# A two-layer decoder step: the score weights and 24 more expert blocks split by ScalarE and GpSimd during the scores

## The chip, the core and the metric

The kernel runs on one core of a Trainium2 chip. The metric is the device time of one execution in microseconds (us). In the profile PE is TensorE's matmul, PEld its weight load, DVE VectorE, ACT ScalarE, POOL GpSimd and SP SyncE, which issues most DMAs.

## What is computed

One inference step of two trunk layers over 512 prompt tokens and 8 sample tokens of width 1024, in float32. Each layer is a token mixer, then a layer norm, then a PEER layer (a mixture of 16384 tiny experts) and a second layer norm. Layer 0 mixes by a gated DeltaNet and an RG-LRU, layer 1 by sliding-window attention. The change lies in PEER:

```python
def block(tb):                                   # 128 tokens
    q = (tb @ w_q).reshape(PEER_BLOCK, PEER_HEADS, 2, PEER_D_SUB)
    s = jnp.einsum('thcd,hcnd->thcn', q, sub_keys).astype(F32)
    s_top, i_top = lax.top_k(s, PEER_TOPK)
    cand = (s_top[:, :, 0, :, None] + s_top[:, :, 1, None, :]).reshape(PEER_BLOCK, PEER_HEADS, -1)
    cand_idx = (i_top[:, :, 0, :, None] * PEER_N_KEYS + i_top[:, :, 1, None, :]).reshape(
        PEER_BLOCK, PEER_HEADS, -1)
    best, pos = lax.top_k(cand, PEER_TOPK)
    expert = jnp.take_along_axis(cand_idx, pos, axis=-1)
    gate = jax.nn.softmax(best, axis=-1)
    act = jax.nn.gelu(jnp.einsum('td,thkd->thk', tb, u_tab[expert]).astype(F32))
    return jnp.einsum('thk,thkd->td', (gate * act).astype(tb.dtype), v_tab[expert])
```

## The kernel before

A float32 product is done in float16 with a **pair**: `hi` is the scaled value rounded to float16 and `lo` the remainder, and `mm3` makes three matmuls, hi by hi, hi by lo and lo by hi. `split` (L73) makes a pair of a block: ScalarE writes `hi` (L71) and VectorE computes `scale * src - hi` in one operation (L80). `wblock` (L89) loads a weight block of 128 by 1024 into a `wst` buffer (three of them) and splits it into `wh` and `wl` (two of each).

`peer` (L271) handles one layer. Three token tiles of 128 (384 tokens) go through TensorE against all 16384 experts, 128 blocks of 128 experts; the fourth tile and the samples (136 columns) gather only the experts chosen. Its stages, in the order of the program:

- **Scores** (L358 to L410). For each of 16 blocks of `wq`: 48 matmuls into `pq`, a copy `q` to SBUF, matmuls against the keys into `psc`, a copy `scs`, and VectorE's top 16 of 128 (`topk_half`).
- **Pairs** (`topk_pairs`, L225). For a list of tokens the sums of the two halves' best are laid out as 50 candidates (`cand`, and `ce` for their expert numbers): 16 operations of VectorE for `cand` and 33 for `ce` (L238, L242), then the top 16 of 50 and a lookup (`eq`). There are six such lists in a layer: the samples, two halves of the gather tile, and three dense tiles.
- **u blocks** (`u_step`, L305). A block of `u` is multiplied with the 384 tokens (24 matmuls into `pu`), and ScalarE applies gelu (`act`). The first 16 blocks of layer 0 (12 of layer 1) were split during the mixer and kept as pairs in DRAM (`PW`, `presplit` L98, `NPRE`); `ublock` (L112) loads those as `wpr` and splits the others through `wblock`. 79 blocks are multiplied before the products with `v` begin.
- **Gather** (L337, L344). GpSimd gathers rows of `u` (36 of 136 in this stretch), and VectorE multiplies and sums each against a token (`hd`, L346).
- **Gates** (L454). For each 32 tokens VectorE builds one-hot rows `oh`, 64 matmuls make `pg`, ScalarE copies them into `stage`, and a DMA of 2 MB writes `GD`; twelve times, with u blocks between.
- **Products** (L613 to L650). 128 blocks of `v` with the gated activations into `yps`, with the rest of the u blocks and gathers between.

The program is built by a scheduler that orders each engine's instructions by a modelled time. So work of a later list, or u blocks, can stand on an engine ahead of work that comes earlier in the text. Once built, the order of each engine is fixed, and an instruction that waits holds up all behind it on its engine.

Of the kernel before, what the change touches and what calls it, by code (L numbers as in the profile page):

```python
# [18 lines left out]
P = 128  # L19
D = 1024  # L20
PB, PC = 4, 2
KB = 8                      # blocks of 128 along d_model
NP = 512                    # prompt tokens
NS = 8                      # sample tokens
NT = NP + NS
ND = 384                    # prompt tokens whose experts go through the tensor engine
W5 = 3 + NP + 4 * NS        # padded sequence of the causal convs
C5 = W5 - 3                 # its outputs
S5 = NP + 3                 # first sample's output column in it (step 4)
# [7 lines left out]
def lookup_order():  # L37
    """pairs (a, b), (a + 1)(b + 1) <= 16, by blocks of product <= 4, 8, 12, 16: segments (a, b0, b1),
    pairs up to each block, and each pair's place in the a-major order of the candidates"""
    start = np.concatenate([[0], np.cumsum([TOPK // (a + 1) for a in range(TOPK)])])  # L40
    seg, cnt, perm = [], [], []
    for hi in (4, 8, 12, 16):
        for a in range(hi):
            b0, b1 = (hi - 4) // (a + 1), hi // (a + 1)
            if b1 > b0:
                seg.append((a, b0, b1))
                perm += [start[a] + b for b in range(b0, b1)]
# [5 lines left out]
SCW = 1024.0                # exact power-of-two scales of the float16 pairs  # L53
# [3 lines left out]
LSC = 8.0 * SQK * SQK       # of the attention's logits  # L57
# [7 lines left out]
class Kern:  # L65
# [3 lines left out]
    # ---------------------------------------------------------------- helpers  # L69
# [3 lines left out]
    def split(self, hi, lo, src, scale=1.0, eng=None):  # L73
        """hi + lo = scale * src, both float16"""
# [7 lines left out]
    def mm3(self, out, wh, wl, xh, xl, start, stop):  # L82
        """out += w^T x of float16 pairs"""
# [5 lines left out]
    def wblock(self, src, lo=None):  # L89
        """one 128-column block of a weight, [128 d, 8, 128] in DRAM, as a scaled float16 pair"""  # L90
# [4 lines left out]
        self.split(h, l, st, SCW, lo)  # L95
        return h, l

    def presplit(self, pool, layer, n):  # L98
        """the first n blocks of u as float16 pairs in DRAM, while a mixer runs"""
# [11 lines left out]
    def ublock(self, layer, b):  # L111
        if b < self.NPRE[layer]:  # L112
# [5 lines left out]
    def proj_block(self, ps, w):  # L118
        """ps[128, 2, 512] (256 + 264 columns) = SCW * w^T x^T"""
# [7 lines left out]
    # ---------------------------------------------------------------- constants  # L127
# [15 lines left out]
    # ---------------------------------------------------------------- layer norm  # L143
# [6 lines left out]
    def layer_norm(self, pool, r, out, gb, n):  # L150
        """out = LN(ALPHA * r) for n tokens on partitions, by halves"""
# [17 lines left out]
    def to_xT(self, psum, src, t, n, tag="s"):  # L169
        """columns of tile t (n tokens) of x^T as a float16 pair"""  # L170
# [1488 lines left out]
```

## Time and profile before

| | |
|---|---|
| device time, 3 runs | 3040.98 us median (3040.34 to 3042.37) |
| span of the profiled execution | 3044.4 us (no other time of it is known) |
| TensorE busy | 2877.3 us, 95% |
| VectorE busy | 2562.9 us, 84% |
| ScalarE busy | 1315.2 us, 43% |
| GpSimd busy | 842.1 us, 28% |
| scores of layer 0 | 368 to 470 us |
| pairs and u blocks of layer 0, up to the first gate matmul | 470 to 625 us |
| gates of layer 0 | 625 to 845 us |
| products of layer 0 | 876 to 1545 us |
| the same points of layer 1 | 1827, 1930, 2098, 2321, 2352, 3034 us |

A row of a group tells line, engine, operation, what it writes and reads, its shape and count, then the engine's busy time and the mean of one, then the idle time just before them and what ended most of it. In a timeline a row has its start, its length and, in brackets, the idle time of its engine before it and what ended that. Matmuls are pipelined: the distance of two starts, not the length, is what one costs.

### The profile page before, as it was taken

The page shows a single profiled execution, that of the slowest core. Times are in us where ns is not written, and L with a number is a line of the kernel's source. Part 1 is how long each engine was busy: PE and PEld are TensorE (multiplying, and loading weights), DVE is VectorE, ACT ScalarE, POOL GpSimd, SP SyncE. Part 2 cuts the span into 40 slices and gives each one's busy share as a digit, 9 for nine tenths or more (in the row PEclk, how much of TensorE's full clock was granted, in tenths as well). Part 3 has the DMA queues.
Part 4 walks back from the last instruction along what each step waited for, and adds up shares of the span by engine and source line. Part 5 has one row for each costly group of instructions (what it writes and reads, how often), then busy time and mean ns, then how long its engine had stood idle before and what let it go on. Part 6 is the DMA issues. An engine that isn't in the chain of part 4 may idle for free.

```text
span 3044.4 us, 49637 instructions
## 1 busy us (share of the span) xinstructions
PE 2877.3 (95%) x18246; PEld 1756.8 (58%) x18246; DVE 2562.9 (84%) x5816; ACT 1315.2 (43%) x2149; POOL 842.1 (28%) x661
## 2 busy tenths in 40 slices
PE   8989999899999999999987899989999999999998
PEld 7787596466655555544455558645665555554443
DVE  6775699999878888899874758989987898888998
ACT  4753232366743333333335633334665333333332
POOL 2300102300045555336410000131001545444552
PEclk9999999999999999999998899999999999999999
DMA  4273326866699999999959512586558999999996
GB/s 134 70 252 112 122 78 223 293 210 214 229 373 374 369 355 364 363 362 365 349 175 231 177 57 91 169 300 223 208 208 307 387 365 357 352 358 354 366 355 239
DMA packets 331689, 798.60 MB, mean 262 GB/s; under 512 B 28515, under 2 KB 164843, under 8 KB 327604
## 3 DMA queue, kind: packets, MB, share of 16 engines
q1 hardware_dynamic: 242832, 444.75, 43.6%
q0 software_dynamic: 78336, 285.25, 25.3%
q10 hardware_dynamic: 10276, 65.43, 5.8%
q8 instruction: 143, 2.34, 0.3%
q14 instruction: 102, 0.84, 0.1%
HBM read 700.89 MB, written 93.10 MB: 261 GB/s over the span
## 4 chain that ended last, share of the span: by engine, by line
PE 61%; DMA 12%; DVE 11%; issue 8%; ACT 6%; POOL 1%; SPq 0%; ACTq 0%; DVEq 0%; POOLq 0%
PE yps L587 30%; PE pu L87 6%; PE pu L86 6%; PE pu L85 6%; DMA GD<-stage 4%; ACT stage L71 3%; DMA row<-in_u_rows,elist 2%; DMA pst<-in_uT 2%; DVE wl L80 2%; DVE row L346 1%; DMA bd<-bt 1%; ACT wh L71 1%; PE pq L85 1%; PE pq L87 1%; PE pq L86 1%
## 5 line engine op out<-in xcount | busy, mean ns | idle before, releaser
L587 PE MATMUL yps<-vv,vw 128*128 128x512 f16 x4536 | 1009.9, 379 | 11.6 <-ACT vv L71 9.9
L587 PEld LDWEIGHTS <-vw 128*128 128x128 f16 x4608 | 450.3, 98 | 543.9 <-issue 17.5
L87 PE MATMUL pu<-xh,wl 128*128 128x384 f16 x1824 | 599.3, 329 | 36.6 <-DVE wl L80 36.2
L339 POOL DMA_INDIRECT row<-in_v_rows,elist x272 | 383.5, 1410 | 891.8 <-ACT stage L71 452.0
L85 PE MATMUL pu<-xh,wh 128*128 128x384 f16 x1824 | 599.7, 329 | 15.7 <-ACT act L315 11.7
L86 PE MATMUL pu<-xl,wh 128*128 128x384 f16 x1824 | 599.6, 329 | 0.0
L71 ACT ACTIVATE wh<-wst 128x1024 f16<-128x1024 f32 x296 | 312.4, 1056 | 606.8 <-PE pu L86 347.7
L339 POOL DMA_INDIRECT row<-in_u_rows,elist x272 | 385.6, 1418 | 674.4 <-DVE hd L346 133.4
L80 DVE SCALAR_TENSOR_TENSOR wl<-wst,wh 128x1024 f16<-128x1024 f32 x296 | 361.2, 1221 | 200.3 <-ACT wh L71 184.7
L87 PEld LDWEIGHTS <-wl 128*128 128x128 f16 x2912 | 288.0, 99 | 186.6 <-DVE wl L80 49.3
L86 PEld LDWEIGHTS <-wh 128*128 128x128 f16 x2912 | 288.2, 99 | 165.9 <-issue 32.0
L85 PEld LDWEIGHTS <-wh 128*128 128x128 f16 x2912 | 290.5, 100 | 158.4 <-ACT wh L71 23.6
L71 ACT ACTIVATE vv<-row 128x1024 f16<-128x1024 f32 x252 | 262.8, 1048 | 222.7 <-PE yps L587 174.7
L525 DVE SCALAR_TENSOR_TENSOR yac<-row,wgt,yac 128x1024 f32<-128x1024 f32 x268 | 343.1, 1280 | 4.3 <-DMA row<-in_v_rows,elist 1.3
L80 DVE SCALAR_TENSOR_TENSOR vv<-row,vv 128x1024 f16<-128x1024 f32 x252 | 307.4, 1221 | 46.3 <-ACT vv L71 41.4
L346 DVE CUSTOM_DVE_ANT_0 row<-row,xtok 128x1024 f32<-128x1024 f32 x256 | 308.5, 1219 | 18.5 <-DMA row<-in_u_rows,elist 18.5
L71 ACT ACTIVATE vw<-act 128x384 f16<-128x384 f32 x256 | 129.8, 516 | 370.4 <-PE yps L587 307.6
L71 ACT ACTIVATE stage<-pg 128x512 f32<-128x512 f32 x192 | 183.4, 1104 | 72.1 <-DMA GD<-stage 67.4
L78 DVE TENSOR_TENSOR vw<-act,vw 128x384 f16<-128x384 f32 x256 | 139.6, 553 | 24.9 <-ACT vw L71 23.3
L315 ACT ACTIVATE act<-pu 128x384 f32<-128x384 f32 x256 | 122.4, 478 | 54.6 <-PE pu L87 41.2
L85 PE MATMUL pq<-xh,wh 128*128 128x264 f16 (+1 forms) x512 | 142.0, 277 | 0.0
L86 PE MATMUL pq<-xl,wh 128*128 128x264 f16 (+1 forms) x512 | 141.9, 277 | 0.0
(482 smaller groups left out, 3997.5 us busy)
## 6 DMA issues: line engine op xcount, KB each, us to landing
row<-in_v_rows SPq DMA_DIRECT2D x256, 512.0 KB
wst<-in_uT SPq DMA_DIRECT2D x228, 512.0 KB
GD<-stage ACTq DMA_DIRECT2D x24, 2048.0 KB
gl<-GD SPq DMA_DIRECT2D x64, 768.0 KB
wst<-in_wq SPq DMA_DIRECT2D x32, 512.0 KB
pst<-in_uT SPq DMA_DIRECT2D x56, 256.0 KB
PW<-ppr SPq DMA_DIRECT2D x56, 256.0 KB
wpr<-PW SPq DMA_DIRECT2D x28, 512.0 KB
```

What stands on the lines that cost most here:

```text
L71: self.nc.scalar.activation(out, in_, AF.Copy, scale=scale)
L78: eng.tensor_sub(lo, src, hi)
L80: eng.scalar_tensor_tensor(lo, src, scale, hi, op0=OP.mult, op1=OP.subtract)
L85: mm(out, wh, xh, start=start, stop=False)
L86: mm(out, wh, xl, start=False, stop=False)
L87: mm(out, wl, xh, start=False, stop=stop)
L315: S.activation(t, ps[:, 0:ND], AF.Gelu_apprx_tanh, scale=1.0 / SCW)
L339: G.indirect_dma_start(out=r, out_offset=None, in_=src, in_offset=bass.IndirectOffsetOnAxis(ap=elist[:, k:k + 1], axis=0))
L346: V.tensor_tensor_reduce(u, u, self.xtok[:, 0] if k < P else xrep, 1.0, 0.0, OP.mult, OP.add, hd[:, k:k + 1])
L525: V.scalar_tensor_tensor(dst, vbuf.pop(n), wgt[:, k:k + 1], dst, op0=OP.mult, op1=OP.add)
L587: T.matmul(yps[t][:, o], w[:, a, c], v[:, b, o], start=x == 0 and k == 0, stop=x == P - 1 and k == 2)
```

## The change

`psplit` is a second way to make a pair. ScalarE writes `hi`, ScalarE scales the source in place, and GpSimd subtracts. All 16 score blocks (`qblock`) use it. During the scores, `presplit_pool` does the same to 24 more blocks of `u`, one or two after each score block: a load of 512 KB into `gst`, two copies of ScalarE, a subtraction of GpSimd, and a DMA of the pair `gpr` to `PW`. So 40 blocks of layer 0 (36 of layer 1) come from DRAM as pairs instead of 16 (12). `sums` lays out the candidates with operations that cover several rows of a: 7 for `cand` and 20 for `ce`.

```diff
+                if seg and seg[-1][1:] == (a, b0, b1):
+                    seg[-1] = (seg[-1][0], a + 1, b0, b1)
+                else:
+                    seg.append((a, a + 1, b0, b1))
...
+CSEG = [(a0, a1, 0, TOPK // a1) for a0, a1 in ((0, 1), (1, 2), (2, 3), (3, 4), (4, 5), (5, 8), (8, 16))]
...
-        self.split(h, l, st, SCW, lo)
+        if lo:
+            self.psplit(h, l, st)
+        else:
+            self.split(h, l, st, SCW)
         return h, l
 
+    def psplit(self, hi, lo, src):
+
+        self.copy(hi, src, SCW)
+        self.copy(src, src, SCW)
+        self.nc.gpsimd.tensor_sub(lo, src, hi)
+
+    def presplit_pool(self, pool, layer, b):
+
+        nc = self.nc
+        st = pool.tile([P, KB, P], F32, name="gst", bufs=2)
+        nc.sync.dma_start(st, self.A["uT"][layer, b])
+        o = pool.tile([P, 2, KB, P], F16, name="gpr", bufs=2)
+        self.psplit(o[:, 0], o[:, 1], st)
+        nc.sync.dma_start(self.PW[layer, b], o)
...
-        if b < self.NPRE[layer]:
+        if b < self.NPRE[layer] + self.NPOOL:
...
-        for a in range(TOPK):
-            nb = TOPK // (a + 1)
-            V.tensor_add(cand[:n, :, off:off + nb], st[:, 0, :, a:a + 1].to_broadcast([n, H, nb]), st[:, 1, :, 0:nb])
-            off += nb
-        off = 0
-        for a, b0, b1 in LSEG:
-            V.tensor_add(ce[:n, :, off:off + b1 - b0], fx[:n, 0, :, a:a + 1].to_broadcast([n, H, b1 - b0]),
-                         fx[:n, 1, :, b0:b1])
-            off += b1 - b0
+
+        def sums(out, x, segs):
+
+            off = 0
+            for a0, a1, b0, b1 in segs:
+                s = [n, H, a1 - a0, b1 - b0]
+                o = out[:n, :, off:off + s[2] * s[3]].rearrange("p h (a b) -> p h a b", a=s[2])
+                V.tensor_add(o, x[:n, 0, :, a0:a1, None].to_broadcast(s), x[:n, 1, :, None, b0:b1].to_broadcast(s))
+                off += s[2] * s[3]
+
+        sums(cand, st, CSEG)
+        sums(ce, fx, LSEG)
...
+            def qblock(hc):
+                return self.wblock(A["wq"][layer, hc], True)
...
-                        wb = self.wblock(A["wq"][layer, hc + 2])
+                        wb = qblock(hc + 2)
...
+                while npool[0] < self.NPOOL * (hc + 1) // 16:
+                    self.presplit_pool(tp, layer, self.NPRE[layer] + npool[0])
+                    npool[0] += 1
...
-            self.NPRE = (16, 12)
-            self.PW = dp.tile([2, max(self.NPRE), P, 2, KB, P], F16, name="PW")
+            self.NPRE, self.NPOOL = (16, 12), 24
+            self.PW = dp.tile([2, max(self.NPRE) + self.NPOOL, P, 2, KB, P], F16, name="PW")
```

The scheduler lays the instructions out anew. ScalarE in the middle of layer 0's scores, one score block before the change (`q` and `scs` are the copies of the projections and of the scores):

```order
L71 ACTIVATE wh<-wst 128x1024
L71 ACTIVATE q<-pq 128x256
L71 ACTIVATE q<-pq 128x264
L71 ACTIVATE scs<-psc 128x512
L71 ACTIVATE ss<-psc 128x8
```

and the same place after it, up to the next block's `wh`:

```order
L76 ACTIVATE wh<-wst 128x1024
L76 ACTIVATE q<-pq 128x256
L76 ACTIVATE q<-pq 128x264
L76 ACTIVATE gst<-gst 128x1024
L76 ACTIVATE scs<-psc 128x512
L76 ACTIVATE ss<-psc 128x8
L76 ACTIVATE wst<-wst 128x1024
L76 ACTIVATE gpr<-gst 128x1024
L76 ACTIVATE gst<-gst 128x1024
L76 ACTIVATE wh<-wst 128x1024
```

The in-place scaling of the score block stands behind the copies of the block before, and one or two u blocks stand between two score blocks.

SyncE's queue at the end of layer 0's scores, before (`wpr` loads a pair, `AD` stores a finished activation):

```order
L92 DMA wst<-in_wq 128x1024 x16
L114 DMA wpr<-PW 128x2048 x4
L317 DMA AD<-act 128x384
L114 DMA wpr<-PW 128x2048
L317 DMA AD<-act 128x384
```

and after (`gst` loads a block to be split, `PW<-gpr` stores it):

```order
L137 DMA wpr<-PW 128x2048
L119 DMA PW<-gpr 128x2048
L116 DMA gst<-in_uT 128x1024
L119 DMA PW<-gpr 128x2048
L116 DMA gst<-in_uT 128x1024
L137 DMA wpr<-PW 128x2048
L119 DMA PW<-gpr 128x2048
L116 DMA gst<-in_uT 128x1024
L342 DMA AD<-act 128x384
L119 DMA PW<-gpr 128x2048
L137 DMA wpr<-PW 128x2048
L342 DMA AD<-act 128x384
```

The loads of the first u blocks now stand behind stores that wait for GpSimd's subtractions.

VectorE ahead of the first one-hot rows `oh` of layer 0, before (`ISA` is the dot product of a gathered row):

```order
L441 CAST ij<-e_6600 128x256
L231 CAST fx_8914<-ix 128x256
L223 MAX_INDEX pos_7757<-best_7756,cwork 128x8
L80 SCALAR_TENSOR_TENSOR wl<-wst,wh 128x1024
L351 TENSOR_TENSOR wgt<-wgt,glist 128x8
L232 TENSOR_SCALAR fx_8914<-fx_8914 128x128
L221 MATCH_REPLACE cwork<-best_7756,cand_7705 128x50
L346 ISA row,hd<-row,xtok 128x1024
L346 ISA hd 128x1
L80 SCALAR_TENSOR_TENSOR wl<-wst,wh 128x1024
L222 MAX best_7756<-cwork 128x8
L448 TENSOR_SCALAR lt<-pt 128x128
```

and after:

```order
L470 TENSOR_SCALAR e_6688<-ei 128x128
L471 TENSOR_SCALAR e_6688<-ei 128x128
L254 CAST fx_8892<-ix 128x256
L244 MATCH_REPLACE cwork<-best_7746,cand_7717 128x50
L371 ISA row,hd<-row,xtok 128x1024
L371 ISA hd 128x1
L473 CAST ij<-e_6688 128x256
L255 TENSOR_SCALAR fx_8892<-fx_8892 128x128
L245 MAX best_7746<-cwork 128x8
L246 MAX_INDEX pos_7747<-best_7746,cwork 128x8
```

The splits `wl` are gone from this place, and work of the next lists stands in theirs.

## Rows read from the trace of the kernel before

**Rows 1.** The page: the span, and busy time by engine

```profile
span 3044.4 us, 49637 instructions
...
PE 2877.3 (95%) x18246; PEld 1756.8 (58%) x18246; DVE 2562.9 (84%) x5816; ACT 1315.2 (43%) x2149; POOL 842.1 (28%) x661
```

**Rows 2.** Busy time by stretch: start:end, length, engines, granted clock, DMA share, GB/s

```profile
368.12:470.00 101.88, 101.88 (x920) 91.49 (x919) 88.13 (x525) 32.41 (x76) 0.00 (x0) 0.99 0.25 79
470.00:625.20 155.20, 138.08 (x813) 79.95 (x811) 142.50 (x635) 49.75 (x76) 49.49 (x38) 0.97 0.82 280
625.20:845.30 220.10, 214.78 (x1799) 146.21 (x1799) 203.83 (x405) 150.19 (x186) 1.87 (x2) 0.99 0.61 215
845.30:876.10 30.80, 24.84 (x142) 13.76 (x140) 19.08 (x22) 16.13 (x23) 8.73 (x6) 0.94 1.00 369
876.10:1545.00 668.90, 662.82 (x3339) 326.10 (x3337) 599.73 (x774) 251.48 (x357) 326.32 (x227) 1.00 1.00 361
1930.00:2098.00 168.00, 147.61 (x861) 85.06 (x860) 153.89 (x657) 55.72 (x83) 50.04 (x38) 0.97 0.78 266
2098.00:2320.90 222.90, 211.03 (x1759) 142.30 (x1757) 197.27 (x387) 147.64 (x183) 2.85 (x3) 0.99 0.60 210
2320.90:2352.20 31.30, 28.73 (x164) 16.04 (x164) 21.14 (x24) 18.42 (x26) 7.30 (x5) 0.95 0.98 367
```

**Rows 3.** Timeline of TensorE around one stall: start, length, engine, line, op, operands, [idle before]

```profile
569.28 0.33 PE L86 MATMUL pu<-xl,wh 128*128 128x384 f16 x1
...
570.26 0.33 PE L86 MATMUL pu<-xl,wh 128*128 128x384 f16 x1
575.76 0.50 PE L87 MATMUL pu<-xh,wl 128*128 128x384 f16 x1 [5.18 <-DVE wl L80]
576.06 0.52 PE L85 MATMUL pu<-xh,wh 128*128 128x384 f16 x1
```

**Rows 4.** The same stall on ScalarE and VectorE

```profile
572.33 1.06 ACT L71 ACTIVATE wh<-wst 128x1024 f16<-128x1024 f32 x1 [5.19 <-DMA wst<-in_uT]
...
572.42 1.23 DVE L346 CUSTOM_DVE_ANT_0 row<-row,xtok 128x1024 f32<-128x1024 f32 x1 [4.38 <-DMA row<-in_u_rows,elist]
```

**Rows 5.** VectorE, 470 to 625 us: groups; busy, mean ns, idle before

```profile
L346 DVE CUSTOM_DVE_ANT_0 row<-row,xtok 128x1024 f32<-128x1024 f32 x28 | 33.8, 1217 | 8.0 <-DMA row<-in_u_rows,elist 8.0
L80 DVE SCALAR_TENSOR_TENSOR wl<-wst,wh 128x1024 f16<-128x1024 f32 x17 | 20.6, 1214 | 1.8 <-ACT wh L71 1.8
...
L242 DVE TENSOR_TENSOR ce<-fx 128x8 f32<-128x8 f32 x53 | 5.6, 169 | 0.0
```

**Rows 6.** Who waited for whom, 470 to 625 us: total us, times, longest

```profile
PE pu L87 <- DVE wl L80: 13.4, 6, 5.6
...
ACT wh L71 <- DMA wst<-in_uT: 7.9, 3, 5.2
```

**Rows 7.** ScalarE, 368 to 470 us: groups

```profile
L71 ACT ACTIVATE wh<-wst 128x1024 f16<-128x1024 f32 x14 | 14.8, 1057 | 59.7 <-PE pq L86 59.7
L71 ACT ACTIVATE scs<-psc 128x512 f32<-128x512 f32 x15 | 9.0, 599 | 0.3 <-PE psc L390 0.3
L71 ACT ACTIVATE q<-pq 128x264 f32<-128x264 f32 x16 | 6.1, 383 | 0.0
```

**Rows 8.** GpSimd, whole span: its largest writes and smallest operations

```profile
L698 POOL MEMSET wbd<- 128x1024 f32 x1 | 1.0, 951 | 0.0
...
masks.py:199 POOL TENSOR_SCALAR_AFFINE_SELECT ident<-ident 128x128 f32<-128x128 f32 x1 | 0.3, 288 | 0.0
...
L1632 POOL MEMSET const-float32-0.0<- 128x1 f32 x1 | 0.1, 104 | 0.3 <-issue 0.3
```

**Rows 9.** GpSimd's copies of the conv state beside VectorE's two-operand split

```profile
L826 POOL COPY cs<-xp x16: 183/972/1188, 29.0 to 152.4; 128x3 f32<-128x3 f32 x16
...
64.67 0.97 POOL L826 COPY cs<-xp 128x3 f32<-128x3 f32 x1 [5.85 <-ACT xp L71]
...
64.38 1.23 DVE L80 SCALAR_TENSOR_TENSOR wl<-wst,wh 128x1024 f16<-128x1024 f32 x1 [1.61 <-ACT wh L71]
```

More of the change, by code (lines that the diff above doesn't have):

```diff
@@ L45, in lookup_order @@
             if b1 > b0:
-                seg.append((a, b0, b1))
+                if seg and seg[-1][1:] == (a, b0, b1):
+                    seg[-1] = (seg[-1][0], a + 1, b0, b1)
+                else:
+                    seg.append((a, a + 1, b0, b1))
                 perm += [start[a] + b for b in range(b0, b1)]
@@ L234, in topk_pairs @@
         ce = pool.tile([P, HM, NC50], F32, name="ce%d" % HM)[:, 0:H]
-        off = 0
-        for a in range(TOPK):
-            nb = TOPK // (a + 1)
-            V.tensor_add(cand[:n, :, off:off + nb], st[:, 0, :, a:a + 1].to_broadcast([n, H, nb]), st[:, 1, :, 0:nb])
-            off += nb
-        off = 0
-        for a, b0, b1 in LSEG:
-            V.tensor_add(ce[:n, :, off:off + b1 - b0], fx[:n, 0, :, a:a + 1].to_broadcast([n, H, b1 - b0]),
-                         fx[:n, 1, :, b0:b1])
-            off += b1 - b0
+        def sums(out, x, segs):
[7 more added lines that the diff above has]
+        sums(ce, fx, LSEG)
         best = pool.tile([P, HM, TOPK], F32, name="best%d" % HM)[:, 0:H]
@@ L371, in proj @@
                 return ps
-            wb = self.wblock(A["wq"][layer, 0])
+            def qblock(hc):
+                return self.wblock(A["wq"][layer, hc], True)
+            wb = qblock(0)
             ps = proj(wb)
-            wb = self.wblock(A["wq"][layer, 1])
+            wb = qblock(1)
+            npool = [0]
             for hc in range(16):
```

## The prediction

> **What bounds the kernel now.** I read the page first, then the busy times by stretch, then the waits and one stall in the timeline. TensorE is busy 2877.3 us of a span of 3044.4 us [rows 1], so a gain can only come from where it stops or runs slowly. In the scores it never stops: 101.9 of 101.9 us. In the products it stops for 6.1 of 668.9 us. What it leaves idle lies between: 17.1 us of the pairs stretch of layer 0 (155.2 less 138.1), 20.4 us in layer 1, 5.3 and 11.9 us in the gates, 6.0 and 2.6 us between the last gate and the first product [rows 2]. To that comes the clock: in both pairs stretches the granted clock is 0.97 [rows 2], so 3% of 155.2 and of 168.0 us, 4.7 and 5.0 us, go to matmuls at the lower level. One stall shows both. TensorE stands still for 5.18 us, waiting for `wl`, the VectorE part of a u block's split, and its next matmuls start 0.30 us apart where six steps before the stall took 0.98 us, 0.163 us each [rows 3]. VectorE is the engine that is late there: it is busy for 142.5 of 155.2 us [rows 2], and 17 splits are 20.6 us of it [rows 5]. But the same stall has a second cause: ScalarE had waited 5.19 us for the block's load, and VectorE 4.38 us for a gathered row [rows 4]. Over the stretch TensorE waited 13.4 us for `wl` and ScalarE 7.9 us for loads [rows 6]. The whole room in the six places is 63.3 us idle and 9.7 us of clock, 73 us. The profiled execution's span is 3.4 us above the median of the runs, 3041.0 us. Nothing else of that execution's own time is known, so I take gains in its microseconds off the median.
>
> **Pairs stretch: the u splits.** The 24 blocks per layer now come as pairs, so TensorE waits there for a load alone. In the new order no split `wl` is left on VectorE ahead of the first one-hot; in layer 0 there were 17, 20.6 us. Ahead of that point stand 113 candidate sums where 196 stood; at 0.169 us [rows 5] the 83 less save 14.0 us. The new sums cover the same elements with more dimensions, which no row prices; at the cost of the old ones apiece the saving is 14.0 us, and at double it would be none. And 27 dots stand ahead instead of 35: eight times 1.217 us [rows 5] is 9.7 us that moves behind. So VectorE has 142.5 - 44.3 = 98 us before the first one-hot, and with the 8.0 us that it waits for rows [rows 5] it would be there at 470 + 106 = 576 us. TensorE is the later one: the new order has 672 u matmuls ahead of the first gate matmul (794 before; layer 1: 683 and 842), 672 x 0.163 = 110 us from 470 us, and with 8 us of waits 588 us, against 625 us before. It has then 122 matmuls, 20 us, less behind it, so the true gain is what it no longer waits. Layer 0: 13.4 us of waits for `wl` and 4.7 us of clock are 18.1 us. The late loads stay: of the 7.9 us on ScalarE [rows 6] I leave 4 us to TensorE, and 14 us are gained. Between what ends: 0, if every stall is a late load, and 21.8 us, if all idle time and the clock come back. Layer 1 has 25.4 us of idle and clock; in the same ratio, 14 of 21.8, it gains 16 us. **Sum 30 us.**
>
> **Gates and the way to the products.** VectorE's work in the gates stays about as it was: 5 splits (6.1 us) and two lists with 22 sums less each (7.4 us) go, 8 dots (9.7 us) come, of 203.8 us [rows 2]. TensorE has 20 us more to do there, and so fewer holes: of 17.2 us idle I take 4 us back; the ends are -6 (VectorE late with the dots) and 17. Behind the last gate stand 168 u matmuls instead of 139 in layer 0, and 150 instead of 164 in layer 1. They cover the store and reload of the gates: 29 x 0.163 = 4.7 us more cover and 2.3 us less. **Plus 2 us.**
>
> **Scores: what comes.** TensorE sets a block's period here, 101.9 / 16 = 6.37 us [rows 2], so whatever fits under it costs nothing. ScalarE gets 14 scalings of `wst` and about 22 pairs of copies; at 1.057 us each [rows 7] that is 58 x 1.057 = 61 us on top of 32.4 us [rows 2], 94 of 101.9 us. It fits by 8 us, in an order where every instruction waits for the one ahead. GpSimd gets 16 + 22 = 38 subtractions of 128 x 1024. No row shows one. The lower end is its write of that size, 0.95 us. For the upper end, an operation that reads 128 elements takes 288 ns and the smallest 104 ns, so 184 ns go to 128 elements; 1024 make 1.47 us, and two operands at twice that with 0.1 us of start 3.05 us [rows 8]. Between 0.95 and 3.05 I take 2.4 us, nearer to the row that reads. Then GpSimd has 38 x 2.4 = 91 us of work in 101.9 us, and from the moment a block's buffers come free `wh` (1.06), two `q` (0.38 each), perhaps a `gst` copy (1.06), `scs` (0.60), the scaling (1.06) and the subtraction (2.4) make 6.9 us, about one period. So ScalarE and GpSimd are both some 90% full, and now and then `wl` comes late. I take 3 us per layer, between 0 and 21 us (38 x 3.05 = 116 us, 14 above the period, and half a period of waiting in turn). SyncE's queue holds the first loads of u behind stores that wait for GpSimd; the old order put 16 score loads and four pairs in a row. Up to two subtractions, 4.8 us, can be late there, which is inside these ends. The first gathers stand behind GpSimd's last subtractions, but wait for the first list anyway. **Minus 6 us.** The 24 MB more of loads and stores per layer go into a stretch with 0.25 of the DMA used [rows 2] and hide there.
>
> [...]
>
> **The sum.** 30 + 4 + 2 - 6 = 30 us: 3041 - 30 = **3011 us**. Nothing is changed in the mixers and the products, which I cost at nothing.
>
> **Rivals.** *Everything hides.* GpSimd is quick, scores cost nothing, and the pairs stretch loses all its idle time and clock: 21.8 + 25.4, with half of the other 25.8 us, are 60 us, 2981 us. For it speaks that `wl` is the wait named; against it the late loads in the same stall.
>
> *VectorE and GpSimd shut each other out.* The trace shows one direction: a copy of GpSimd that takes 0.18 us alone took 0.97 us when VectorE's split of two SBUF operands had begun 0.29 us before it, and it ended with that split [rows 9]. If it also holds the other way, a VectorE operation with two operands waits for a whole subtraction. By the new order 27 sums of the first half of the gather tile stand in the middle of the scores, with subtractions all around. At 2.4 us each they take 65 us. VectorE has 13.8 us free there [rows 2] and 17 us from the splits that left: it falls 34 us behind if nothing brakes it, and 19 us if its three `scs` buffers stop ScalarE, and with it GpSimd, after three blocks. The first one-hot then comes at 595 to 610 us instead of 588, and each layer loses 7 to 22 us: 3025 to 3055 us, in the middle 3040 us. Against it: the top-16 operations, most of VectorE's work there, read one operand.
> [...]
>
> *GpSimd sets the scores (slower).* If a subtraction takes more than 101.9 / 38 = 2.7 us, GpSimd becomes the bound of the scores, and each 0.1 us above costs 3.8 us per layer. The other terms give 36 us, so from (101.9 + 18) / 38 = 3.15 us on the kernel is slower than before. At 3.6 us it costs 35 us per layer: 3041 - 36 + 70 = 3075 us. Mixed types (float32 less float16, into float16) and waits for VectorE speak for it; the rows end at 3.05 us.
>
> *Late loads keep the stalls.* The u loads in the pairs stretch share the DMA with 36 gathers, at 0.82 of the DMA and 280 GB/s where 361 is the most of a long stretch [rows 2]; the stretch gets shorter and its bytes hardly fewer. Then the splits leave and the stalls stay: 8 us of the 30 are gained, 3033 us.
>
> **How the numbers follow.** Forecast 0.46, everything hides 0.18, shut out 0.14, GpSimd bound 0.15, late loads 0.07. A measurement of this kernel tells about 0.2%, 6 us, from no change: faster is below 3035 us. Faster: 0.46 + 0.18 + 0.04 of the lock + 0.05 of the late loads = 0.73; within: 0.08 of the lock and 0.02 of the late loads and 0.01, 0.11; slower 0.16. The range goes from 2972 us, under the first rival by the rest of the room in the gates, to 3045 us, which leaves out GpSimd bound and the worst of the lock.
>
> **What would show it.** In the scores: the length of GpSimd's subtractions (0.95 to 3.05), TensorE's idle time (3 us expected), whether `pq` waits for GpSimd or for ScalarE, and the length of the candidate sums beside a subtraction (0.17 alone). In the pairs stretch: no wait for `wl`, the first gate matmul near 591 us, loads `wpr` as the wait that ends last. In the gates: idle about 13 us in both. I am wrong if a subtraction takes over 3.15 us, or if the first gate matmul comes after 605 us.

## The result and the profile after

The changed kernel takes 3063.1 us in the median (3055.0 to 3063.4), the kernel before 3040.7 us: a ratio of 1.0070 (95% interval 1.0057 to 1.0084), so it is slower by some 22 us, 0.7%. The forecast was 3011 us, faster, with 3045 us as the end of its range.

The page of the changed kernel, its span and busy time by engine, beside [rows 1]:

```profile
span 3061.6 us, 49672 instructions
...
PE 2883.0 (94%) x18246; PEld 1759.7 (57%) x18246; DVE 2470.0 (81%) x5472; ACT 1395.4 (46%) x2229; POOL 1012.6 (33%) x741
```

VectorE lost 93 us of work, as meant, and TensorE does as much as before in a longer span. Where the time went stands in the stretches. The busy times by stretch, columns as in [rows 2]; the rows are scores, pairs stretch and gates of layer 0, then of layer 1, then the products of layer 1:

```profile
370.30:483.50 113.20, 106.44 (x925) 92.37 (x923) 76.84 (x491) 86.13 (x130) 72.68 (x35) 0.97 0.79 264
483.50:611.40 127.90, 115.71 (x687) 68.11 (x687) 111.04 (x535) 38.62 (x62) 43.63 (x35) 0.97 0.87 303
611.40:838.90 227.50, 211.02 (x1758) 141.75 (x1757) 192.37 (x360) 133.47 (x167) 10.90 (x11) 1.00 0.66 230
...
1842.60:1956.00 113.40, 106.30 (x928) 92.69 (x927) 74.05 (x465) 86.22 (x129) 71.96 (x34) 0.97 0.76 260
1956.00:2084.20 128.20, 117.52 (x695) 68.77 (x694) 117.37 (x570) 38.51 (x62) 45.44 (x35) 0.97 0.87 303
2084.20:2301.80 217.60, 208.72 (x1767) 142.03 (x1767) 197.10 (x359) 139.63 (x175) 9.42 (x10) 1.00 0.68 240
...
2334.00:3050.90 716.90, 706.92 (x3557) 348.38 (x3555) 617.61 (x799) 259.43 (x365) 318.23 (x229) 1.00 0.95 338
```

From the last score projection to the first gate matmul, the pairs stretches are 28 and 41 us shorter than before, and the kernel is still slower. Lengths mislead here, because u blocks move between stretches: the pairs stretch has 135 and 176 matmuls of u less than before, and the products have 133 and 164 more. TensorE makes them all the same. What can be gained or lost is what a stretch takes above its matmuls. So from here on a stretch's **loss** is its time, from start to start of its matmuls, less their count times what one costs where TensorE is never held up (0.1625 us for u, 0.0574 for gates, 0.1108 for the score projections, 0.103 for the scores, 0.2158 for the products). It holds the stops and the slower clock together. A second profile of the kernel before (the last run below, span 3031.9 us) shows how far such numbers repeat: each within 3 us, though the two spans differ by 12.5 us in all.

Left of a slash stands layer 0, right of it layer 1; the gain is over both layers, from the mean of the two profiles before.

| loss, us | before (two profiles) | after | forecast gain | measured gain |
|---|---|---|---|---|
| scores, layer 0 / 1 | 1.2, 1.7 / 2.1, 0.8 | 11.4 / 11.0 | -6 | -19.5 |
| pairs stretch | 23.9, 23.2 / 29.4, 28.0 | 18.0 / 17.2 | +30 | +17.1 |
| gates | 8.9, 5.9 / 18.5, 18.8 | 23.4 / 11.6 | +4 | -9.0 |
| last gate to first product | 8.3, 8.8 / 4.7, 3.6 | 3.6 / 8.0 | +2 | +1.1 |
| products | 8.5, 8.5 / 8.1, 6.7 | 8.3 / 16.1 | 0 | -8.5 |

The sum is -18.8 us; with 2.7 us that the scores start later and 1.5 us in the mixer of layer 1 it is 23 us, against 22 us measured.

**Scores.** GpSimd's subtractions (the line of the subtraction, both uses; count, shortest, median, longest in ns):

```profile
L110 POOL TENSOR_TENSOR gpr<-gst,gpr x48: 2122/2135/2182, 376.6 to 1971.7; 128x1024 f16<-128x1024 f32 x48
L110 POOL TENSOR_TENSOR wl<-wst,wh x32: 2119/2134/2153, 360.3 to 1948.0; 128x1024 f16<-128x1024 f32 x32
```

One took 2.13 us, 2.12 to 2.18 in all 80, so GpSimd is busy for only 72.7 of 113.2 us. Still TensorE stops. Who waited for whom in the scores of layer 0 (total us, times, longest):

```profile
ACT gpr L76 <- DMA gst<-in_uT: 22.1, 12, 3.3
...
PEld L92 <- POOL wl L110: 8.4, 6, 2.4
PE pq L92 <- POOL wl L110: 6.7, 6, 2.2
```

One of these stops in the timeline (start, length, operation, in brackets the idle time before it), ScalarE first, then GpSimd, then TensorE:

```profile
394.10 1.04 ACT L76 ACTIVATE wh<-wst 128x1024 f16<-128x1024 f32 x1
395.05 0.64 ACT L76 ACTIVATE q<-pq 128x256 f32<-128x256 f32 x2
395.58 1.05 ACT L76 ACTIVATE gst<-gst 128x1024 f32<-128x1024 f32 x1
396.52 0.59 ACT L76 ACTIVATE scs<-psc 128x512 f32<-128x512 f32 x1
...
397.06 1.07 ACT L76 ACTIVATE wst<-wst 128x1024 f32<-128x1024 f32 x1
399.47 1.06 ACT L76 ACTIVATE gpr<-gst 128x1024 f16<-128x1024 f32 x1 [1.33 <-DMA gst<-in_uT]
...
396.76 2.14 POOL L110 TENSOR_TENSOR gpr<-gst,gpr 128x1024 f16<-128x1024 f32 x1 [2.38 <-issue]
398.85 2.13 POOL L110 TENSOR_TENSOR wl<-wst,wh 128x1024 f16<-128x1024 f32 x1
...
401.04 0.36 PE L92 MATMUL pq<-xh,wl 128*128 128x256 f16 x1 [2.17 <-POOL wl L110]
```

Between `wh` and the scaling of `wst`, on which the subtraction depends, stand the copies of the block before and a scaling for a u block, 2 us. GpSimd then finishes the u block first. `wl` is there 5.8 us after `wh`, and TensorE waits 2.17 us for it. Behind it ScalarE waits 1.33 us for the next u block's load, and the next `wh` stands behind that. Over the stretch ScalarE is busy for 86.1 us and waits 22.1 us for such loads: the two fill 108 of its 113.2 us.

**Pairs stretch.** No wait for `wl` is left, as forecast. Another one grew: ScalarE's wait for the softmax of a list, with the gelu (`act`) of finished u blocks behind it. Who waited for whom, 483.5 to 611.4 us:

```profile
ACT L277 <- DVE gexp L276: 19.0, 3, 9.2
...
PE pu L90 <- ACT act L340: 10.8, 4, 5.3
```

Before, the same two were 5.7 us and 2.9 us. The longest of them in the timeline of ScalarE, VectorE and TensorE:

```profile
565.47 1.28 ACT L277 ACT_TABLE_LOAD   x1 [9.15 <-DVE gexp L276]
566.76 0.31 ACT L277 ACTIVATE gexp<-gexp 128x128 f32<-128x128 f32 x1
567.09 1.28 ACT L340 ACT_TABLE_LOAD   x1
568.38 0.49 ACT L340 ACTIVATE act<-pu 128x384 f32<-128x384 f32 x1
...
565.11 0.28 DVE L276 TENSOR_TENSOR gexp<-best 128x128 f32<-128x128 f32 x1
...
568.92 0.48 PE L90 MATMUL pu<-xh,wpr 128*128 128x384 f16 x1 [5.34 <-ACT act L340]
569.19 0.53 PE L91 MATMUL pu<-xl,wpr 128*128 128x384 f16 x1
```

ScalarE stands 9.15 us for VectorE, then loads a table for the exponential and another to return to gelu, 1.28 us each. Both `pu` buffers are full by then. It is the stall of [rows 3] over again, 5.34 us instead of 5.18, with the matmuls behind it 0.3 us apart, and with another wait that ends last.

**Gates.** ScalarE in late gate stages: first before the change, layer 0 and then layer 1, then layer 0 after the change. A stage is eight copies out of `pg` in two rows of four, then the store of 2 MB from the one `stage` buffer:

```profile
808.44 3.74 ACT L71 ACTIVATE stage<-pg 128x512 f32<-128x512 f32 x4 [3.64 <-DMA GD<-stage]
811.97 1.07 ACT L71 ACTIVATE wh<-wst 128x1024 f16<-128x1024 f32 x1
812.93 0.49 ACT L315 ACTIVATE act<-pu 128x384 f32<-128x384 f32 x1
813.29 3.78 ACT L71 ACTIVATE stage<-pg 128x512 f32<-128x512 f32 x4
817.10 0.33 ACTq L478 DMA_DIRECT2D GD<-stage  x1
...
824.32 3.75 ACT L71 ACTIVATE stage<-pg 128x512 f32<-128x512 f32 x4 [4.00 <-DMA GD<-stage]
...
2279.88 3.71 ACT L71 ACTIVATE stage<-pg 128x512 f32<-128x512 f32 x4 [6.10 <-DMA GD<-stage]
...
2289.83 0.33 ACTq L478 DMA_DIRECT2D GD<-stage  x1
...
2297.83 3.71 ACT L71 ACTIVATE stage<-pg 128x512 f32<-128x512 f32 x4 [6.11 <-DMA GD<-stage]
```

```profile
744.10 3.72 ACT L76 ACTIVATE stage<-pg 128x512 f32<-128x512 f32 x4 [5.68 <-DMA GD<-stage]
747.62 1.05 ACT L76 ACTIVATE wh<-wst 128x1024 f16<-128x1024 f32 x1
748.57 0.48 ACT L340 ACTIVATE act<-pu 128x384 f32<-128x384 f32 x1
748.93 1.06 ACT L76 ACTIVATE wh<-wst 128x1024 f16<-128x1024 f32 x1
749.88 0.50 ACT L340 ACTIVATE act<-pu 128x384 f32<-128x384 f32 x1
750.25 3.79 ACT L76 ACTIVATE stage<-pg 128x512 f32<-128x512 f32 x4
754.07 0.33 ACTq L510 DMA_DIRECT2D GD<-stage  x1
...
762.03 3.72 ACT L76 ACTIVATE stage<-pg 128x512 f32<-128x512 f32 x4 [6.07 <-DMA GD<-stage]
```

The work is the same, six u operations (three `wh`, three `act`) a stage. Before, in layer 0, four of them lie under the store, where ScalarE has to wait anyway, and two between the copies. After, it is two and four. The round of copies, store and copies is the period: 8.66 us from the first copy to the store and 7.22 us until the buffer is free, 15.9 us; and 9.97 + 7.96 = 17.9 us. So 1.3 of the 2 us are the two operations more between the copies. The other 0.7 us are a store that takes longer; why it does was not followed. TensorE's own work in it is 72 matmuls of u and 64 of gates, 15.4 us. I call the two orders 4+2 and 2+4. Before, the late stages of layer 0 are 4+2 and those of layer 1 are 2+4; after the change it is the other way round, with seven stages of the slow kind in a row where layer 1 had four. Over all stages layer 0 loses 16 us more than before and layer 1 loses 7 less.

### The profile page after: what moved, and what is told of

It reads as the page before. It is cut to its first block, busy times and chain, and to the rows that moved or that the text cites. A ratio compares the mean times of both kernels' runs of the same rounds, so it can differ in the third digit from the quotient of the medians.

```text
span 3061.6 us, 49672 instructions
## 1 busy us (share of the span) xinstructions
PE 2883.0 (94%) x18246; PEld 1759.7 (57%) x18246; DVE 2470.0 (81%) x5472; ACT 1395.4 (46%) x2229; POOL 1012.6 (33%) x741
## 4 chain that ended last, share of the span: by engine, by line
PE 49%; DMA 20%; DVE 12%; ACT 9%; issue 6%; POOL 2%; SPq 0%; ACTq 0%; DVEq 0%; POOLq 0%
PE yps L619 21%; PE pu L92 5%; PE pu L90 5%; PE pu L91 5%; DMA GD<-stage 5%; ACT stage L76 4%; DMA row<-in_u_rows,elist 3%; DMA gst<-in_uT 3%; DMA row<-in_v_rows,elist 2%; DVE row L371 2%; DMA gl<-GD 2%; DMA pst<-in_uT 2%; ACT wh L76 2%; POOL row L364 1%; DMA wst<-in_wc 1%
## 5 line engine op out<-in xcount | busy, mean ns | idle before, releaser
L619 PE MATMUL yps<-vv,vw 128*128 128x512 f16 x4536 | 1008.7, 380 | 15.9 <-DVE vv L85 12.8
L364 POOL DMA_INDIRECT row<-in_u_rows,elist x272 | 364.4, 1340 | 465.5 <-DVE hd L371 161.6
L90 PE MATMUL pu<-xh,wh 128*128 128x384 f16 x1440 | 470.6, 327 | 17.0 <-ACT act L340 12.9
L92 PE MATMUL pu<-xh,wl 128*128 128x384 f16 x1440 | 469.7, 327 | 5.4 <-DVE wl L85 5.4
L91 PE MATMUL pu<-xl,wh 128*128 128x384 f16 x1440 | 470.4, 327 | 0.0
L76 ACT ACTIVATE wh<-wst 128x1024 f16<-128x1024 f32 x248 | 261.1, 1054 | 316.7 <-PE pu L91 203.9
L85 DVE SCALAR_TENSOR_TENSOR wl<-wst,wh 128x1024 f16<-128x1024 f32 x216 | 263.7, 1223 | 173.9 <-ACT wh L76 167.0
L557 DVE SCALAR_TENSOR_TENSOR yac<-row,wgt,yac 128x1024 f32<-128x1024 f32 x268 | 343.3, 1281 | 23.3 <-DMA row<-in_v_rows,elist 21.3
L91 PEld LDWEIGHTS <-wh 128*128 128x128 f16 x2528 | 250.1, 99 | 141.5 <-issue 30.2
L90 PEld LDWEIGHTS <-wh 128*128 128x128 f16 x2528 | 252.4, 100 | 137.4 <-ACT wh L76 24.9
L92 PEld LDWEIGHTS <-wl 128*128 128x128 f16 x2528 | 250.2, 99 | 135.3 <-POOL wl L110 13.6
L90 PE MATMUL pu<-xh,wpr 128*128 128x384 f16 x608 | 200.7, 330 | 22.6 <-ACT act L340 19.9
L91 PE MATMUL pu<-xl,wpr 128*128 128x384 f16 x608 | 200.5, 330 | 0.0
L92 PE MATMUL pu<-xh,wpr 128*128 128x384 f16 x608 | 200.5, 330 | 0.0
```

Of the source, the lines that this page charges most:

```text
L76: self.nc.scalar.activation(out, in_, AF.Copy, scale=scale)
L85: eng.scalar_tensor_tensor(lo, src, scale, hi, op0=OP.mult, op1=OP.subtract)
L90: mm(out, wh, xh, start=start, stop=False)
L91: mm(out, wh, xl, start=False, stop=False)
L92: mm(out, wl, xh, start=False, stop=stop)
L364: G.indirect_dma_start(out=r, out_offset=None, in_=src, in_offset=bass.IndirectOffsetOnAxis(ap=elist[:, k:k + 1], axis=0))
```

## The experiments

"Loss" is as above, for layer 0 and then layer 1. A ratio is against runs of the kernel before made beside it, with its 95% interval. A loss is read from one profile of each kernel.

**The sums alone.** Changed kernel without the rest:

```
-                return self.wblock(A["wq"][layer, hc], True)
+                return self.wblock(A["wq"][layer, hc])
...
-            self.NPRE, self.NPOOL = (16, 12), 24
+            self.NPRE, self.NPOOL = (16, 12), 0
```

> Only the candidate sums in fewer operations: the score weights are split on VectorE as before, and no u block is added to those that come as pairs. VectorE has 22 sums less in each list, 3.7 us at 0.169 us, so about 15 us less ahead of the first gate matmul and 22 us per layer in all. Theory A (VectorE's lateness in the pairs stretch is what TensorE waits for): the stops of the pairs stretch, 17.1 and 20.4 us before, fall by about 8 us each, and the time by 10 to 20 us, to some 3026 us. Theory B (what is saved on VectorE comes back as another wait, as in the changed kernel, where the pairs stretch still stops for 12.2 and 10.7 us and the gates stop for longer): within 5 us of 3041 us.

Measured: 3046.0 us, 1.0022 (1.0010 to 1.0035): slower than before by some 7 us, so theory A is out and theory B holds at its edge. The pairs stretches lose 28.4 and 25.2 us, together what they lost before, and the late gate stages have turned to 2+4 in layer 0 (loss 23.3) and to 4+2 in layer 1 (11.5). So the turn in the gates came with the sums, not with the splits.

**Score blocks back on VectorE**, u blocks as changed:

```
-                return self.wblock(A["wq"][layer, hc], True)
+                return self.wblock(A["wq"][layer, hc])
```

> The changed kernel, but the 16 score blocks of a layer are split on VectorE, as before the change; the 24 u blocks stay with ScalarE and GpSimd. Theory A (the scores lose their 11 and 9 us because the score block's own lo part comes from GpSimd, 2.13 us behind a scaling of 1.06 us and behind a u subtraction): the scores run at 102 us again, TensorE stops for under 1 us there, and the time is some 19 us below the changed kernel, 3044 us or less. Theory B (the loss comes from the u blocks that stand in ScalarE's and GpSimd's fixed order, waiting for their loads): the scores stay at 108 us or more. Rival on VectorE: its splits of two operands now stand beside 24 subtractions and each can wait for one, up to 2.1 us more apiece; then VectorE is late with wl and the scores are 115 us or more.

Measured: 3089.3 us, 1.0160 (1.0142 to 1.0178). The scores lose 16.5 and 13.3 us, so theory A is not the whole of it. ScalarE waited 39.3 us for loads of u blocks in layer 0. TensorE's stops there are 6.5 us for `scs`, a copy of ScalarE, and one of 2.3 us for VectorE's `wl`: the scores of layer 0 are 116 us long, as the rival gave, but not for its reason. The profile is that of the slowest of its executions (3102.8 us), and its 33.4 us of loss in the products of layer 1 were not followed.

**No u blocks in the scores**, score blocks with ScalarE and GpSimd:

```
-            self.NPRE, self.NPOOL = (16, 12), 24
+            self.NPRE, self.NPOOL = (16, 12), 0
```

> The changed kernel with none of the 24 u blocks: the score blocks are split by ScalarE and GpSimd, the sums are the new ones, and u is split on VectorE in the pairs stretch as before. Theory A (the score block's own chain through GpSimd is slow): the scores stay at 108 us or more with 16 subtractions of 2.13 us. Theory B (the u blocks in the fixed order make the loss): the scores are back at 102 to 103 us. The pairs stretch keeps its 17 splits on VectorE. The time by A some 3040 us or more, by B 3015 to 3035 us, by what the first run shows for the sums.

Measured: 3050.7 us, 1.0035 (1.0023 to 1.0048). The scores of layer 0:

```profile
370.40:471.60 101.20, 101.20 (x911) 90.66 (x910) 73.72 (x491) 44.87 (x87) 29.82 (x14) 0.99 0.24 79
```

TensorE never stops. With 16 subtractions and nothing of u between them the chain over GpSimd costs nothing, so theory A falls and the u blocks make the loss. The time is above what B gave: the gates are those of the sums alone (22.5 and 10.5 us).

**Three buffers for the loads:**

```
-        st = pool.tile([P, KB, P], F32, name="gst", bufs=2)
+        st = pool.tile([P, KB, P], F32, name="gst", bufs=3)
```

> The changed kernel with three buffers instead of two for the loads of the u blocks, so that a load can begin one block earlier. In the changed kernel ScalarE waited 22.1 us (12 times, up to 3.3 us) in the scores of layer 0 for these loads, with the score block's wh behind it. Theory B (late loads at the head of ScalarE's order make the loss of the scores): ScalarE's wait for the loads falls under 6 us, TensorE's stops in the scores from 6.8 us to under 2 us, and the time by 10 to 15 us, to 3050 us. Theory A (GpSimd's own time sets it): the waits move to GpSimd and the time stays within 4 us of 3063 us.

Measured: 3052.8 us, 1.0046 (1.0029 to 1.0062). The time is as theory B said, its reason is not: ScalarE's wait for loads fell from 22.1 to 2.2 us, yet the scores lose 14.6 and 10.6 us. ScalarE now waits for the pairs' stores (11.8 us), and TensorE for GpSimd's `wl` (10.1 us). The 10 us were gained in the pairs stretches (12.1 and 12.1 us of loss, 11 less than in the changed kernel).

**The old sums** in the changed kernel:

```
             for a0, a1, b0, b1 in segs:
-                s = [n, H, a1 - a0, b1 - b0]
...
+                for a in range(a0, a1):
+                    s = [n, H, b1 - b0]
+                    V.tensor_add(out[:n, :, off:off + b1 - b0], x[:n, 0, :, a:a + 1].to_broadcast(s), x[:n, 1, :, b0:b1])
+                    off += b1 - b0
```

> The changed kernel with the candidate sums as before the change, 49 operations a list; the score blocks and the 24 u blocks stay with ScalarE and GpSimd. In the order of ScalarE the late gate stages of layer 0 now have four of its six u operations (two wh, two act) under the store of the stage and two between the copies, as in layer 0 before the change, and those of layer 1 two and four, as layer 0 of the changed kernel. Theory G (a gate stage of the second kind takes 18.0 us instead of 15.9 us, whatever else was changed, since one stage buffer's round of store and copies sets the time): the time over the matmuls' own rate in the gates is about 9 us in layer 0 and about 18 us in layer 1, where the changed kernel had 23 and 12 us. The pairs stretch gets 83 x 0.169 = 14 us of VectorE work back ahead of the first gate matmul. If VectorE sets its end that is 14 us more per layer and the time is 3075 us or more; if what is saved on VectorE only becomes another wait, within 6 us of 3063 us.

Measured: 3061.5 us, 1.0067 (1.0045 to 1.0089), no different from the changed kernel. The gates lose 14.0 and 22.2 us: the layers have changed places, as the order said, at 4 to 5 us above the forecast losses. The 22 sums less in each of six lists, 22 us of VectorE per layer, move the whole kernel by nothing that shows.

**Twelve u blocks** instead of 24:

```
-            self.NPRE, self.NPOOL = (16, 12), 24
+            self.NPRE, self.NPOOL = (16, 12), 12
```

> The changed kernel with 12 u blocks per layer in the scores instead of 24, so one after three of four score blocks. The late gate stages have four u operations of ScalarE under the store and two between the copies in both layers. Theory B (u blocks ahead of a score block in ScalarE's fixed order make the loss of the scores): the scores lose under 5 us per layer over the matmuls' own rate, where they lose 11.4 and 11.0 us with 24. Theory G: the gates lose about 9 to 12 us in both layers, where they lose 23.4 and 11.6 us. Both together give 3035 to 3045 us. If neither holds, the time is between those with no u block (3051 us) and 24 (3063 us).

Measured: 3037.7 us, 0.9994 (0.9980 to 1.0008), level with before. The scores lose 8.8 and 4.9 us, more in layer 0 than expected; the gates 13.4 and 11.2 us. The schedule did not spread the 12 blocks: in layer 0 all their subtractions begin before 435 us, and so do TensorE's three stops for `wl`, while the scores run to 477 us.

**Three buffers each** for loads and pairs:

```
-        st = pool.tile([P, KB, P], F32, name="gst", bufs=2)
+        st = pool.tile([P, KB, P], F32, name="gst", bufs=3)
...
-        o = pool.tile([P, 2, KB, P], F16, name="gpr", bufs=2)
+        o = pool.tile([P, 2, KB, P], F16, name="gpr", bufs=3)
```

> The changed kernel with three buffers each for the loads and for the pairs of the u blocks in the scores. With three for the loads alone ScalarE's waits moved to the stores of the pairs, 11.8 us in layer 0. Theory B in its first form (waits of ScalarE for buffers and loads make the loss of the scores): both waits go, and the scores lose under 4 us per layer over the matmuls' own rate. Theory B in a second form (the loss is that wl of the score block waits in GpSimd's fixed order behind a subtraction of a u block): the loss stays at 8 us or more and TensorE's waits name GpSimd's wl. Theory G: in this order the late gate stages of both layers have two u operations under the store and four between the copies, so the gates lose 20 us or more in both layers, 18.0 us a stage.

Measured: 3065.3 us, 1.0080 (1.0062 to 1.0097). The scores lose 13.1 and 13.6 us with no wait for stores left, and TensorE's stops are waits for GpSimd's `wl`, 7.8 and 7.4 us: what the second form of B says, the place in GpSimd's order. But ScalarE still waits 10.8 and 10.1 us for loads, so the first form is not shut out. The pairs stretches lose 12.8 and 11.6 us, 28 us less than before, nearly the forecast; in layer 0 the wait for the softmax is 12.4 us there instead of 19.0 and TensorE's wait for `act` 3.7 instead of 10.8. The gates are 2+4 in both layers and lose 22.8 and 24.5 us.

**The same with the old sums** (both edits above):

> As the run with three buffers each, but with the candidate sums as before the change. In this order the late gate stages of both layers have four u operations of ScalarE under the store and two between the copies. Theory G: a stage takes 15.9 us, the gates lose 9 to 13 us in both layers, some 20 us less in all than in the run with three buffers and new sums, although VectorE has 22 sums more per list. Rival (VectorE's work sets the pairs stretch and the gates): this kernel is slower than that one by 20 to 30 us, 22 x 0.169 x 6 = 22 us per layer. The scores as in that run.

Measured: 3061.1 us, 1.0071 (1.0054 to 1.0089). The late stages take 15.9 us in both layers; the gates lose 16.1 and 17.8 us, 13 us less than in the run before, not 20. The early stages took up to 26 us, 24 in the run before. The rival is out: with 22 sums more a list the kernel is not slower than the one with three buffers.

**Score blocks on VectorE and three buffers each:**

```
-                return self.wblock(A["wq"][layer, hc], True)
+                return self.wblock(A["wq"][layer, hc])
...
+        st = pool.tile([P, KB, P], F32, name="gst", bufs=3)
...
+        o = pool.tile([P, 2, KB, P], F16, name="gpr", bufs=3)
```

> Score blocks split on VectorE as before the change, the 24 u blocks with ScalarE and GpSimd, with three buffers each for their loads and pairs; new sums. It is the fourth corner beside the changed kernel (two buffers, wl on GpSimd: the scores of layer 0 lose 11.4 us over the matmuls' own rate), the run with wl on VectorE (two buffers: 16.5 us) and the run with three buffers each (wl on GpSimd: 13.1 us). Theory B2 (the loss has two causes, each enough by itself: ScalarE's order waits for the u blocks' loads and buffers, and wl stands behind u subtractions in GpSimd's order): here both are gone, and the scores lose under 4 us per layer. Rival L (VectorE's two-operand split waits for whole subtractions of GpSimd, up to 2.1 us each): the scores lose 8 us or more and TensorE waits for wl of VectorE. By the order of ScalarE the late gate stages have four u operations under the store in both layers: 15.9 us a stage, and gates that lose 9 to 14 us. The time: 3010 to 3030 us by B2, 3035 us or more by L.

Measured: 3029.5 us, 0.9967 (0.9956 to 0.9978): faster than both kernels. The scores of layer 0:

```profile
373.20:478.00 104.80, 102.04 (x912) 90.63 (x910) 89.19 (x450) 79.21 (x122) 52.44 (x24) 0.98 0.86 313
```

The loss is 5.2 and 5.5 us, between the two theories. Neither edit alone helped the scores and both together halved the loss, as B2 says, though the waits are less and not gone: ScalarE still waits 17.4 and 15.0 us for loads. Of what stays, TensorE's stops are 1.8 and 3.1 us for `scs` of ScalarE, and 1.0 us in layer 0 alone for VectorE's `wl`, which is all that shows of rival L. Two of the splits of VectorE (wl) and the subtractions of GpSimd beside them:

```profile
415.13 2.14 POOL L110 TENSOR_TENSOR gpr<-gst,gpr 128x1024 f16<-128x1024 f32 x1 [1.22 <-ACT gst L76]
422.73 2.13 POOL L110 TENSOR_TENSOR gpr<-gst,gpr 128x1024 f16<-128x1024 f32 x1 [1.37 <-ACT gst L76]
...
415.98 2.37 DVE L85 SCALAR_TENSOR_TENSOR wl<-wst,wh 128x1024 f16<-128x1024 f32 x1 [0.54 <-ACT wh L76]
422.95 2.98 DVE L85 SCALAR_TENSOR_TENSOR wl<-wst,wh 128x1024 f16<-128x1024 f32 x1
```

Clear of a subtraction a split took 1.2 us (at 402.2 and 408.9 us). These two took 2.37 and 2.98 us: both began inside a subtraction and ended 1.1 us after it, so they waited until GpSimd was done. Of the 14 splits in this stretch seven took 1.2 us and seven 1.8 to 2.98 us. The gates are 4+2 in both layers and lose 6.3 and 13.4 us.

**The same with twelve u blocks:**

> As the run with score blocks on VectorE and three buffers each, with 12 u blocks per layer instead of 24. Theory B2: the scores lose under 2 us per layer; the pairs stretch loses 14 to 20 us per layer, a few us more than with 24, since splits of u are left on VectorE. The late gate stages have four u operations under the store in both layers (15.9 us). The time 3015 to 3030 us. Rival L: VectorE's splits wait for half as many subtractions, the scores lose 4 us or more, and the time is 3035 us or more.

Measured: 3040.0 us, 0.9999 (0.9987 to 1.0011). A miss. The scores lose 1.8 and 2.6 us, as B2 said, and the late gate stages take 15.9 us, but the gates of layer 0 lose 21.1 us: two of the early stages took 27.7 and 23.2 us. Which wait is late there was not followed.

**The sums, and two more blocks split in the mixer:**

```
-                return self.wblock(A["wq"][layer, hc], True)
+                return self.wblock(A["wq"][layer, hc])
...
-            self.NPRE, self.NPOOL = (16, 12), 24
+            self.NPRE, self.NPOOL = (18, 12), 0
```

> Only the new candidate sums, as in the run of the sums alone, and two more u blocks of layer 0 split during the mixer (18 instead of 16), which shifts the order. In the run of the sums alone five late gate stages of layer 0 had two u operations under the store and took 18.2 us each; here all late stages of both layers have four. Theory G: the gates of layer 0 lose 9 to 13 us over the matmuls' own rate instead of 23 us, and the time is some 10 to 15 us below the run of the sums alone: 3030 to 3037 us, which is also below the kernel before. Rival (the gates of layer 0 lose time because VectorE comes to them earlier, whatever the order): they lose 20 us or more again, and the time stays at 3042 us or more.

Measured: 3032.3 us, 0.9974 (0.9961 to 0.9987): 14 us below the sums alone, and faster than before. The gates lose 6.0 and 10.3 us. Two blocks more are 2.4 us of VectorE's work; the gates of layer 0 alone lose 17 us less.

**The kernel before again:**

> The kernel before the change once more, for a second profile: the stretches of two executions of one program show how far a difference of a stretch can be read. By the order the gates of layer 0 and layer 1 lose about 9 and 18 us again, the pairs stretches about 24 and 29 us; a span of 3033 to 3045 us.

Measured: a span of 3031.9 us; gates 5.9 and 18.8, pairs stretches 23.2 and 28.0 us. The span is 1 us below what was expected. The table above has it.

**Two readings over all runs.** The late gate stages, the last four periods of each layer in all 14 profiles, from store to store: 72 of the kind 4+2, 15.8 to 16.7 us, mean 16.0; 40 of the kind 2+4, 17.1 to 19.3 us, mean 18.0. They don't overlap. From the first copy to the store a stage of the second kind takes 9.9 us for 8.7, from the store to the next copy 8.1 us for 7.3. And the scores:

| score blocks' `wl` on | u blocks | buffers, load and pair | loss, us |
|---|---|---|---|
| GpSimd | 0 | | 1.5 / 2.0 |
| GpSimd | 12 | 2, 2 | 8.8 / 4.9 |
| GpSimd | 24 | 2, 2 (the change) | 11.4 / 11.0; with the old sums 10.3 / 12.5 |
| GpSimd | 24 | 3, 2 | 14.6 / 10.6 |
| GpSimd | 24 | 3, 3 | 13.1 / 13.6; with the old sums 13.5 / 11.7 |
| VectorE | 24 | 2, 2 | 16.5 / 13.3 |
| VectorE | 24 | 3, 3 | 5.2 / 5.5 |
| VectorE | 12 | 3, 3 | 1.8 / 2.6 |

## Why the prediction was wrong

**Pairs stretch, forecast +30, measured +17.** Right: no wait for `wl`, and the gain grows to 28 us when loads and pairs get a third buffer. Wrong: the sum took the late loads as the only thing left. It asked what is late next on TensorE (its own count of matmuls) and not on ScalarE, whose order holds the exponential of each list ahead of the gelus. With VectorE still the late engine, that wait went from 5.7 to 19.0 us in layer 0. No run changed that order alone. The first gate matmul came at 611 us; 591 was forecast and 605 named as the point from which I am wrong. Of the 20 us, 11 are the later end of the scores: 2 a later start, 9 a length beyond the 3 us forecast.

**Scores, forecast -6, measured -19.5.** The price of a subtraction was good (2.13 us for 2.4, between 0.95 and 3.05 by [rows 8]). The step that failed is the one after it: 91 us of work in 101.9 us was taken to mean "now and then late", 3 us a layer, and the loads and stores of the u blocks to "hide there". GpSimd had less to do than that, 72.7 us in layer 0, and the scores lost 10 us a layer. The load alone does not tell it: in ScalarE's fixed order and in GpSimd's a score block's operations stand behind those of a u block, and a u block's stand behind its load. The prediction had added up such a chain, 6.9 us against a period of 6.37, and then priced it as slack. Nor did the loads hide: ScalarE, whose 94 us of work were to fit by 8 us, had 86.1 us of work and 22.1 us of waits for them. Without u blocks the loss is gone; how it divides between the order on ScalarE, the order on GpSimd and the waits for loads stays open, since no run changed one of them alone. The wide end it gave, 21 us a layer, held.

**Gates, forecast +4, measured -9.** The step counted VectorE's work, and that did fall (192.4 us for 203.8 in layer 0). The late stages are set by the round of the one `stage` buffer on ScalarE, and what moves them is which u operations stand under the store. What sets the early ones, up to 31 us long in other runs, was not followed. The lists ahead of the prediction show ScalarE's order only in the scores; in the gates they would have shown 2+4 and 4+2, with both prices in the trace of before: 15.9 us a stage in layer 0, 18.0 in layer 1. The trace of before and the new order were enough to see this ahead.

**Last gate to first product** came out as said. **Products** were costed at nothing: right for layer 0; in layer 1 8.5 us more are lost, 10.0 us of stops for 5.5 (four of over 0.7 us, the longest 3.9). Most of them, 6.9 us, are waits for VectorE's half of a split of `v`; before they were for ScalarE's. Why VectorE comes late there stays open.

**The rivals.** *GpSimd sets the scores* ended on the right side by the wrong mechanism: a subtraction, with its mixed types, took 2.13 us, far below the 2.7 at which it would be the bound. *VectorE and GpSimd shut each other out*, which the chances call the lock, is real, but no wait of TensorE for it shows in the scores here. VectorE in the middle of layer 0's scores, then GpSimd:

```profile
447.51 2.16 DVE L254 CAST fx<-ix 128x128 f32<-128x128 uint32 x1
...
450.69 1.66 DVE L265 TENSOR_TENSOR ce<-fx 128x16 f32<-128x16 f32 x20
...
447.46 2.12 POOL L110 TENSOR_TENSOR wl<-wst,wh 128x1024 f16<-128x1024 f32 x1
452.77 2.14 POOL L110 TENSOR_TENSOR gpr<-gst,gpr 128x1024 f16<-128x1024 f32 x1 [3.19 <-ACT gst L76]
```

The cast waited out the subtraction, and two sums of the seven for `cand` took 2.1 and 1.4 us. The 20 sums for `ce` fell into a pause of GpSimd and took 1.66 us together, not 2.4 us each; and VectorE waits 36 us for `scs` there anyway. *Late loads keep the stalls* is wrong: in the pairs stretches TensorE waits 0.2 us for `wpr` in layer 0 and 1.5 us in layer 1. *Everything hides* fell with the scores.

**What a version should take.** The best run here leaves the score blocks on VectorE and gives the u blocks a third buffer: 11 us below before. It keeps the gain in the pairs stretch (15.7 and 15.4 us of loss), pays 5 us a layer in the scores, and has the fast gate order in both layers, the last by chance of the schedule.

## What to carry to other kernels

An engine that is 64% busy (GpSimd in the scores) can still be the one that is late: when work is handed to idle engines, write down the order that each will hold and follow one block through it, with its loads, before adding up the load. Count what a stretch loses above its matmuls, not its length, since a scheduler moves the matmuls elsewhere. And where a ring of one buffer sets a period, look at which work the order puts under its store and which between its fills: the same six operations were worth 2 us a stage, and with all late stages of layer 0 turned round its gates lost 17 us less.

## What was not expected of the hardware

GpSimd's subtraction of 128 by 1024 (float32 less float16, into float16) took 2.12 to 2.18 us in all 80 of its runs in the changed kernel. The exclusion of [rows 9] showed the other way too: in the run with score blocks on VectorE and three buffers each VectorE's two-operand split took 2.98 us for 1.2, and in the changed kernel a sum of 128 by 16 took 2.1 us for 0.17. A cast with one operand, begun 0.05 us after a subtraction, waited as well, 2.16 us where the same cast took 0.22 us in the kernel before. The top-16 operations hardly notice: in the scores of layer 0 their search for the places (FIND_INDEX8) took 0.288 us on the mean for 0.281.
